# One decoder layer on one core: bias rows copied to the output early, the last token tile stored plainly, two chunks split ahead in the value product

## The chip, the cores and the metric

One core of one Trainium2 chip runs the whole layer. TensorE (PE) multiplies, VectorE (DVE), ScalarE (ACT) and GpSimd (POOL) work on tiles, SyncE (SP) issues most of the transfers; POOL issues those that add to what is already at the destination. The metric is the time of one execution in microseconds (us), the median of several; less is better.

## The reference

One layer: a mixer (dilated attention and a spatial gating unit), cross-attention into 256 memory tokens, and a SwiGLU block, each added to alpha times the stream and normalised. Width 2048, 512 tokens, hidden width 5632, all in float32. The change touches the end of the second part and the third:

```python
def _memory_cross_attention(h, mem, w_q, w_k, w_v, w_o):
    q = (h @ w_q).reshape(B, S, XATTN_HEADS, XATTN_HEAD_DIM)
    k = (mem @ w_k).reshape(B, M, XATTN_HEADS, XATTN_HEAD_DIM)
    v = (mem @ w_v).reshape(B, M, XATTN_HEADS, XATTN_HEAD_DIM)
    s = jnp.einsum('bshe,bmhe->bhsm', q, k).astype(jnp.float32) * (XATTN_HEAD_DIM ** -0.5)
    p = jax.nn.softmax(s, axis=-1)
    o = jnp.einsum('bhsm,bmhe->bshe', p.astype(v.dtype), v).reshape(B, S, D)
    return o @ w_o
...
    h = _layer_norm(DEEPNORM_ALPHA * h + xa, ln2_g[l], ln2_b[l])
    ff = (jax.nn.silu(h @ w_ffn_gate[l]) * (h @ w_ffn_up[l])) @ w_ffn_down[l]
    h = _layer_norm(DEEPNORM_ALPHA * h + ff, ln3_g[l], ln3_b[l])
```

## The kernel before

Every float32 product is made of three matmuls: each operand is split into a high part (a cast on ACT) and a low part (a subtraction on DVE), and high x high, high x low and low x high are added in PSUM. Weights come in chunks of 1 MB. All code is in one function; the order of the instructions on every engine is the order in which the program writes them, with small generators (a `Sched` that resumes them at every `tick()`) to interleave side work. Each engine runs its own instructions strictly in that order.

**The value product** (lines 1278 to 1315). The products of the memory's values with the output weights were made earlier and lie in DRAM (`vo_d`). So what is left of the cross-attention is a product of the attention weights `xpt` with 16 chunks, numbered 0 to 15 here: two halves of the tokens (`hf`), four column blocks (`cb`), two chunks each (`kb`). For a chunk c, `w_load` brings 1 MB into one of two raw buffers (`wraw`), and `w_split` makes two casts (line 199, into `whi`) and two subtractions (line 200, into `wlo`); `whi` and `wlo` have two buffers each. `next_w(c)` calls `w_ahead(c)`, which splits chunk c + 1 and loads c + 2 and c + 3, and only then come the 24 matmuls of chunk c (lines 235 to 237). Behind every second chunk two results are added to the residual on DVE (line 1307, the residual comes from DRAM into the single tile `Xa`) and their statistics taken (line 1308). After chunk 7 the first token half is normalised by `ln2(0)`: a chain of small DVE instructions (lines 382 to 385), then activations on ACT (line 1016) and POOL. `first_half` then transposes and splits that half (lines 1028 to 1049).

**SwiGLU.** Eleven blocks (j = 0 to 10) of 28 items each make the gate and up products by a seven-product (Strassen) scheme, P1 to P7, then six blocks make the down product. `Feed` keeps the weights coming: `pump` loads half-megabyte tiles `T` and `rt` on SP's queue up to 10 items ahead, `a` casts, `b` subtracts (lines 1198 and 1205) into one of four `ws` tiles; where a sum of two weight blocks is wanted, `b` lets POOL load the second block with an addition (line 1212). `prime` makes the first three of these splits, at the start of chunk 14 (line 1299).

**The end.** `gbs` (line 1546) loads the gain and bias rows of the last norm, repeated over 128 partitions, as soon as the tile of P2's operand is free, and then writes the bias rows four times into the output (line 1553), 1 MB each. The last results of P6 are added on DVE (line 1367) in the queue behind the last four splits, and PE's last two products (P7, P4) use P6's banks, so they wait for that. `final_ln` normalises a token tile on ACT (line 1541), multiplies by the gain on DVE (line 1542), and POOL adds the result onto the bias rows in DRAM (line 1543).

Of the kernel before, what the change touches and what calls it, by code (L numbers as in the profile page):

```python
# [17 lines left out]
P = 128  # L18
D = 2048
# [20 lines left out]
def layer_kernel(tc, x, mem, positions, ln_in_g, ln_in_b, w_in, sgu_norm_g, sgu_norm_b,  # L40
# [14 lines left out]
    def pool(name, stack=ctx, bufs=1, **kw):  # L55
        kw.setdefault("reuse_waits", "tile")
        if kw.get("space") == DRAM:
            kw.pop("reuse_waits")
        return stack.enter_context(tc.tile_pool(name=name, bufs=bufs, **kw))
# [9 lines left out]
    psa = pool("psa", space=PSUM)  # L69
    pst = ExitStack()  # L70
    psx = pool("psx", pst, space=PSUM)

    def acc():
        return psa.tile([P, 512], F32, name="acc", bufs=4)
# [108 lines left out]
    def w_tiles(c):  # L183
        if c < 21 and c % 3 == 2:
            q = [actp.tile([P, 2, 512], F32R, name=f"act{12 + j}").rearrange("p a b -> p (a b)") for j in range(4)]
            return q[:2], q[2:]
        hi = wp.tile([P, 2048], F32R, name="whi", bufs=2)
        lo = wp.tile([P, 2048], F32R, name="wlo", bufs=2)
        return ([hi[:, 0:1024], hi[:, 1024:2048]], [lo[:, 0:1024], lo[:, 1024:2048]])
# [21 lines left out]
    def w_ahead(c):  # L211
        w_load(c + 1)
        w_split(c + 1)
        if c < 19:
            w_load(c + 2)
            w_split(c + 2)
        w_load(c + 2)
        w_load(c + 3)
# [154 lines left out]
    def bcast(ap, n):  # L373
        return bass.AP(tensor=ap.tensor, offset=ap.offset, ap=[[0, P], [1, n]])
# [582 lines left out]


    phe = ExitStack()
    pf = [None, None]  # L960

    def open_e():
        ph.close()
# [45 lines left out]
    def ln2(hf):  # L1009
        ts = (2 * hf, 2 * hf + 1)  # L1010
        ln_chain(ts, stat2, mv2)
        for c in (0, 2, 1, 3):
            for t in ts:
                o = y2[t, c]
                if c < 2:
                    A.activation(o, o, AF.Identity, bias=mv2[:, t, 3:4], scale=mv2[:, t, 2:3])
                else:
                    G.tensor_scalar(o, o, mv2[:, t, 2:3], mv2[:, t, 3:4], op0=OP.mult, op1=OP.add)
        for c in range(4):
            for t in ts:  # L1020
                G.dma_start(y2n_d[t][c], y2[t, c])
# [219 lines left out]
                self.b()  # L1241
            self.pump()

    NR, NW = 4, 4
    feed = Feed()

    def half_rows(w, r, c0):
# [30 lines left out]
    for hf in range(2):  # L1278
        for cb in range(4):
            ps, rs = None, None  # L1280
            for kb in range(2):
                if kb == 0 and hf + cb == 0:
                    sched.need(lambda: 0 in xpt and 1 in xpt)
                if kb == 1 and hf + cb == 0:
                    sched.need(lambda: 2 in xpt and 3 in xpt)
                wh, wl = next_w(f"xo{hf}_{cb}", kb)
                if kb == 0:
                    ps = [acc() for _ in range(2)]
                if kb == (1 if hf + cb == 0 else 0):
                    if not y2:  # L1290
                        new_y2()
                    rs = zt("Xa")
                    for u in range(2):
                        nc.sync.dma_start(rs[:, u], res_d[1][2 * hf + u][:, cb * 512:cb * 512 + 512])
                    if hf == 1 and cb == 1:
                        feed.pump(4)
                    if hf == 1 and cb == 3:
                        feed.pump()
                        feed.prime()
                for i in range(2):  # L1300
                    t = 2 * hf + i
                    ts = slice(t * 128, t * 128 + 128)
                    for k in range(4):
                        x_ = xpt[(kb * 4 + k) // 2][:, k % 2]
                        mm3(ps[i], x_[:, 0, ts], x_[:, 1, ts], wh[:, k], wl[:, k], kb + k == 0, kb == 1 and k == 3)
                    if kb == 1:
                        V.tensor_tensor(y2[t, cb], ps[i], rs[:, i], OP.add)
                        V.bn_stats(stat2[:, t, cb], y2[t, cb])
                        if cb == 3 and i == 1:
                            ln2(hf)  # L1310
                            if hf == 0:
                                new_comb(A11)
                                new_comb(A12)
                                sched.spawn(first_half(), 4)
                    tick()
# [133 lines left out]
    for j in range(FB):  # L1449
        x = {}  # L1450

        def on(name, bk, j=j, x=x):
            def c11(bank_a, bank_d):
                for i in range(2):
                    V_ADD(x[1][:, i], bank_d[i], x[1][:, i])
                A.activation(x[1], x[1], AF.Silu)

            def x1(bank_a):
                x[1] = zt("Xa")
                for i in range(2):  # L1460
                    A.copy(x[1][:, i], bank_a[i])

            if name == "P1":
                x["A"] = bk
                if j:
                    x1(bk)
            elif name == "P2":
                if j == 0:
                    x1(x["A"])
                c11(x["A"], bk)  # L1470
                if 1 <= j <= 8:
                    sched.spawn(residual_task(j - 1), 1)
            elif name == "P5":
                x["H"] = zt("XH")
                x[5], x[12] = x["H"][:, 0:2], x["H"][:, 2:4]
                for i in range(2):
                    A.copy(x[5][:, i], bk[i])
            elif name == "P3":
                x["B"] = bk
            elif name == "P6":  # L1480
                x[2] = zt("Xb")
                for i in range(2):
                    A.copy(x[2][:, i], bk[i])

                def c12():
                    yield 1
                    for i in range(2):
                        V_ADD(x[12][:, i], x["B"][i], x[2][:, i])
                    V.tensor_tensor(x[12], x[12], x[1], OP.mult)
                    yield 2  # L1490
                    if j == FB - 1:
                        load_y("Xa", [(0, 0), (1, 0)])
                    x["fc"] = zt("FC")
                    yield from ff_first(j, x["fc"], x[12])
                sched.spawn(c12(), 0)
            elif name == "P7":
                for i in range(2):
                    V_ADD(x[2][:, i], bk[i], x[2][:, i])
                V_ADD(x[5], x[5], x[2])
            elif name == "P4":  # L1500
                for i in range(2):
                    V_ADD(x[2][:, i], bk[i], x[2][:, i])
                A.activation(x[2], x[2], AF.Silu)

                def rest():
                    V.tensor_tensor(x[5], x[5], x[2], OP.mult)
                    yield 2
                    yield from ff_second(j, x["fc"], x[5])
                sched.spawn(rest(), 1)
            if j == FB - 1:  # L1510
                next_group(0, name)

        def gate(name, c, j=j):
            if j == 0 and name not in ("P1", "P2"):
                sched.need(lambda: built[0] > c)
        product_block(*plan[j], on, gate if j == 0 else None)
# [18 lines left out]
    def final_ln(*ts):  # L1535
        ln_chain(ts, stat3, mv3)
        for c in (2, 3, 1, 0):
# [5 lines left out]
                G.dma_start(out[t * 128:(t + 1) * 128, z], o, accum_op=OP.add)  # L1543
            yield 1

    def gbs():
        yield 1
        for i, s_ in enumerate((ln3_g[0], ln3_b[0])):
            gb3.append(pf[0].tile([P, D], F32, name=f"c{A12}_{i}"))
            nc.sync.dma_start(gb3[i], bcast(s_, D))  # L1550
        yield 3
        for t in range(NT):
            nc.sync.dma_start(out[t * 128:(t + 1) * 128, :], gb3[1])

    for g in range(3):
        for nb in range(2):
# [48 lines left out]
            if last and nb:  # L1605
                cut = [o for o in order if o[0] in ("P7", "P4")]
                bank = product_block(n, order[:-len(cut)], on)
                assert feed.nb == len(feed.items)
                for name in ("P7", "P4"):
                    ws = [feed.next((name, c)) for c in range(n)]  # L1610
                    for i in range(2):
                        for c in range(n):
                            mm_item(bank["P6"], COMB[name], c, ws[c], False, c == n - 1, (i,))
                            if c < n - 1:
                                tick()
                        acc_y(2 + i, n1 if name == "P7" else n0, bank["P6"][i], True)
                        if name == "P4":
                            sched.spawn(final_ln(2 + i), 1)
                        tick()
            else:  # L1620
                product_block(n, order, on)
# [45 lines left out]
```

## Time and profile before

| | |
|---|---|
| Time, median of 3 runs | 2631.56 us (2630.79 to 2632.6) |
| The profiled execution: its own time | 2631.51 us |
| its span, first to last instruction | 2629.5 us |
| PE busy | 2550.6 us, 97% |
| DVE, ACT, POOL busy | 1726.2, 1104.4, 235.7 us |
| Mean granted TensorE clock | 0.989 of 2.4 GHz |

PE is the engine that sets the time: in the long middle of the kernel it has no gap at all. Its busy time is a sum of records that overlap (a matmul of 512 columns has a record of 0.39 us and a start every 0.227 us), so what is lost is better read from the starts than from the share.

### The profile page before, as it was taken

The numbers are of one execution on the slowest core, as the hardware profiler recorded it, in microseconds if no ns is written. First come the engines' busy times: TensorE is split into PE (matmuls) and PEld (weight loads), VectorE is DVE, ScalarE is ACT, GpSimd is POOL, SyncE is SP. The second block draws the span as 40 slices with busy tenths as digits, with TensorE's granted clock in tenths as the row PEclk, the third lists the DMA queues.
The fourth block names the chain that finished last, engine by engine and source line by source line (L and its number), as shares of the span: only waits on it lengthen the run. The fifth ranks groups of instructions, "written<-read, shape, count | busy, mean of one in ns | idle before, by whom it ended". The sixth has DMA issues, their size and how long they took to land.

```text
span 2629.5 us, 31646 instructions
## 1 busy us (share of the span) xinstructions
PE 2550.6 (97%) x12421; PEld 2146.8 (82%) x12421; DVE 1726.2 (66%) x2216; ACT 1104.4 (42%) x1370; POOL 235.7 (9%) x256
## 2 busy tenths in 40 slices
PE   8999999999999999998989999999999999999994
PEld 8999888888888888886778888888888877888883
DVE  4766556474535456435787777778777768787785
ACT  4464433233332134223655554545555544333432
POOL 1311000000000010001211111111110100000022
PEclk9999999999999999999999999999999999999997
DMA  8769722323334233425848888878888799887977
GB/s 295 235 202 306 220 80 81 96 66 108 87 105 181 96 112 113 150 91 180 260 118 230 236 242 245 202 224 225 234 239 240 202 348 304 286 273 224 287 195 168
DMA packets 271252, 511.80 MB, mean 195 GB/s; under 512 B 14464, under 2 KB 68992, under 8 KB 263680
## 3 DMA queue, kind: packets, MB, share of 16 engines
q1 hardware_dynamic: 223120, 411.15, 46.2%
q0 software_dynamic: 44336, 91.83, 17.6%
q10 hardware_dynamic: 3648, 6.82, 0.7%
q8 instruction: 97, 1.59, 0.2%
q14 instruction: 51, 0.42, 0.1%
HBM read 431.62 MB, written 78.12 MB: 194 GB/s over the span
## 4 chain that ended last, share of the span: by engine, by line
PE 43%; DMA 4%; DVE 4%; issue 2%; ACT 1%; POOL 1%; SPq 0%; POOLq 0%; DVEq 0%; ACTq 0%
PE acc L1342 10%; PE acc L1343 10%; PE acc L1341 10%; PE D L1342 4%; PE D L1343 4%; PE D L1341 4%; DMA Xa<-res_d 2%; DVE ws L1205 1%; PE aux L1396 1%; DMA T<-in_w_ffn_down_dram 1%; DVE wlo L200 1%; POOL out_dram L1543 1%; DMA rt<-in_w_ffn_gate_dram 0%; DVE T L1184 0%; DMA rt<-in_w_ffn_down_dram 0%
## 5 line engine op out<-in xcount | busy, mean ns | idle before, releaser
L200 DVE TENSOR_TENSOR wlo<-wraw,whi 128x1024 fp32r<-128x1024 f32 x258 | 305.1, 1225 | 264.1 <-ACT whi L199 263.8
L1198 ACT CAST ws<-T 128x1024 fp32r<-128x1024 f32 x263 | 275.7, 1054 | 395.4 <-PE acc L1343 110.8
L199 ACT CAST whi<-wraw 128x1024 fp32r<-128x1024 f32 x258 | 258.2, 1050 | 326.3 <-PE acc L237 195.5
L1205 DVE TENSOR_TENSOR ws<-T,ws 128x1024 fp32r<-128x1024 f32 x263 | 317.3, 1222 | 92.0 <-ACT ws L1198 91.6
L1205 DVE TENSOR_TENSOR ws<-rt,ws 128x1024 fp32r<-128x1024 f32 x195 | 237.9, 1222 | 80.9 <-ACT ws L1198 80.5
L1198 ACT CAST ws<-rt 128x1024 fp32r<-128x1024 f32 x195 | 205.0, 1054 | 187.8 <-PE acc L1343 145.6
L1343 PE MATMUL acc<-ws,big 128*128 128x512 f32 x528 | 207.1, 392 | 3.8 <-DVE big L1061 3.8
L1341 PE MATMUL acc<-ws,big 128*128 128x512 f32 x528 | 206.9, 392 | 2.1 <-ACT big L1058 2.1
L1342 PE MATMUL acc<-ws,big 128*128 128x512 f32 x528 | 206.8, 392 | 1.6 <-DVE ws L1205 1.5
L235 PE MATMUL acc<-whi,act 128*128 128x512 f32 x512 | 201.3, 393 | 0.0
L237 PE MATMUL acc<-whi,act 128*128 128x512 f32 x512 | 199.4, 390 | 0.0
L236 PE MATMUL acc<-wlo,act 128*128 128x512 f32 x512 | 199.2, 389 | 0.0
L235 PE MATMUL acc<-act,whi 128*128 128x512 f32 x384 | 152.0, 396 | 0.0
L237 PE MATMUL acc<-act,wlo 128*128 128x512 f32 x384 | 149.8, 390 | 0.0
L236 PE MATMUL acc<-act,whi 128*128 128x512 f32 x384 | 149.5, 389 | 0.0
L235 PE MATMUL acc<-memT,whi 128*128 128x256 f32 x432 | 122.4, 283 | 4.5 <-ACT whi L199 3.2
L237 PE MATMUL acc<-memT,wlo 128*128 128x256 f32 x432 | 122.0, 282 | 1.7 <-DVE wlo L200 1.6
L236 PE MATMUL acc<-memT,whi 128*128 128x256 f32 x432 | 121.1, 280 | 0.0
L1343 PEld LDWEIGHTS acc<-ws,big 128*128 128x128 f32 x528 | 99.9, 189 | 25.7 <-DVE big L1061 5.1
L1341 PEld LDWEIGHTS acc<-ws,big 128*128 128x128 f32 x528 | 99.8, 189 | 23.5 <-ACT big L1058 2.8
L1342 PEld LDWEIGHTS acc<-ws,big 128*128 128x128 f32 x528 | 99.8, 189 | 23.4 <-DVE ws L1205 2.7
L237 PEld LDWEIGHTS acc<-whi,act 128*128 128x128 f32 x512 | 96.1, 188 | 20.2
(396 smaller groups left out, 5952.9 us busy)
## 6 DMA issues: line engine op xcount, KB each, us to landing
rt<-in_w_ffn_gate_dram SPq DMA_DIRECT2D x88, 512.0 KB, 6.0
rt<-in_w_ffn_down_dram SPq DMA_DIRECT2D x82, 512.0 KB, 7.3
wraw<-in_w_in_dram SPq DMA_DIRECT2D x40, 1024.0 KB, 5.8
T<-in_w_ffn_gate_dram SPq DMA_DIRECT2D x44, 512.0 KB, 3.9
T<-in_w_ffn_up_dram POOLq DMA_DIRECT2D x44, 512.0 KB, 11.0
rt<-in_w_ffn_up_dram SPq DMA_DIRECT2D x44, 512.0 KB, 8.4
rt<-in_w_ffn_up_dram POOLq DMA_DIRECT2D x44, 512.0 KB, 6.2
wraw<-in_w_xv_dram SPq DMA_DIRECT2D x16, 1024.0 KB, 6.8
```

The source lines that it names most:

```text
L199: A.copy(hi[s], r[:, z])
L200: V.tensor_tensor(lo[s], r[:, z], hi[s].bitcast(F32), OP.subtract)
L235: T.matmul(o, lh, rh, start=start, stop=False)
L236: T.matmul(o, lh, rl, start=False, stop=False)
L237: T.matmul(o, ll, rh, start=False, stop=stop)
L1198: A.copy(e["ws"][:, 0], self.tiles[e["src"]])
L1205: V.tensor_tensor(e["ws"][:, 1], self.tiles[e["src"]], e["ws"][:, 0].bitcast(F32), OP.subtract)
L1341: T.matmul(bank[i], lh, rh, start=start and kk == 0, stop=False, skip_group_check=True)
L1342: T.matmul(bank[i], lh, rl, start=False, stop=False, skip_group_check=True)
L1343: T.matmul(bank[i], ll, rh, start=False, stop=stop and kk == 1, skip_group_check=True)
L1396: T.transpose(p[:, kk * 256 + i * 128:kk * 256 + i * 128 + 128], x[:, i, f * 128:f * 128 + 128], ident)
L1543: G.dma_start(out[t * 128:(t + 1) * 128, z], o, accum_op=OP.add)
```

## The change

Three things are altered. (1) The four writes of the bias rows at the end go away; instead SP copies the bias vector from DRAM, repeated 128 times, straight to three of the four row blocks of the output, one 1 MB transfer in each of the first three SwiGLU blocks, behind P2. (2) The fourth token tile gets its own closing function, `final_last`: gain and bias are both applied on chip (for two of the four column blocks DVE does it all in two instructions, for the other two ACT normalises first), and SP stores the result plainly. (3) In the value product, from chunk 1 on, `w_ahead` splits two chunks ahead, every third chunk into two of the `ws` tiles in place of `whi` and `wlo`; one more `w_ahead` stands in front of `ln2(0)`; and `prime` comes one chunk later.

```diff
@@ w_tiles
+        if c >= NCH - 14 and (c - NCH + 16) % 3 == 2:
+            t = [pf[0].tile([P, 2, 1024], F32R, name="ws", bufs=NW) for _ in range(2)]
+            return tuple([q[:, 0], q[:, 1]] for q in t)
@@ w_ahead
-        if c < 19:
+        if c < 19 or c >= NCH - 15:
             w_load(c + 2)
             w_split(c + 2)
@@ the value product
-                    if hf == 1 and cb == 3:
-                        feed.pump()
-                        feed.prime()
+                if hf == 1 and cb == 3 and kb == 1:
+                    feed.pump()
+                    feed.prime()
...
                         if cb == 3 and i == 1:
+                            if hf == 0:
+                                w_ahead(pos[0])
                             ln2(hf)
@@ SwiGLU blocks, behind P2
+                if j < 3:
+                    nc.sync.dma_start(out[j * 128:(j + 1) * 128, :], bcast(ln3_b[0], D))
@@ the end
+    def final_last(t):
+        ln_chain((t,), stat3, mv3)
+        rows = slice(t * 128, t * 128 + 128)
+        for c in (0, 1):
+            o = y[t, c]
+            A.activation(o, o, AF.Identity, bias=mv3[:, t, 3:4], scale=mv3[:, t, 2:3])
+        for c in (2, 0, 3, 1):
+            z = slice(c * 512, (c + 1) * 512)
+            o = y[t, c]
+            if c > 1:
+                V.scalar_tensor_tensor(o, o, mv3[:, t, 0:1], gb3[0][:, z], op0=OP.subtract, op1=OP.mult)
+                V.scalar_tensor_tensor(o, o, mv3[:, t, 2:3], gb3[1][:, z], op0=OP.mult, op1=OP.add)
+            else:
+                V.tensor_tensor(o, o, gb3[0][:, z], OP.mult)
+                V.tensor_tensor(o, o, gb3[1][:, z], OP.add)
+            nc.sync.dma_start(out[rows, z], o)
+        yield 1
...
-        yield 3
-        for t in range(NT):
-            nc.sync.dma_start(out[t * 128:(t + 1) * 128, :], gb3[1])
...
-                            sched.spawn(final_ln(2 + i), 1)
+                            sched.spawn(final_ln(2) if i == 0 else final_last(3), 1)
```

DVE at the start of the value product, before; `wlo<-wraw,whi` are splits (x2 is one chunk: first chunk 2, then 3 and 4), `Xb` and `XH` take the first and the second column block's results:

```order
L200 TENSOR_TENSOR wlo<-wraw,whi 128x1024 x2
L1307 TENSOR_TENSOR Xb<-acc,Xa 128x512
L1308 BN_STATS stat<-Xb 128x6
L1307 TENSOR_TENSOR XH<-acc,Xa 128x512
L1308 BN_STATS stat<-XH 128x6
L200 TENSOR_TENSOR wlo<-wraw,whi 128x1024 x4
L1307 TENSOR_TENSOR Xb<-acc,Xa 128x512
```

The same place now:

```order
L206 TENSOR_TENSOR ws<-wraw,ws 128x1024 x2
L206 TENSOR_TENSOR wlo<-wraw,whi 128x1024 x2
L1311 TENSOR_TENSOR Xb<-acc,Xa 128x512
L1312 BN_STATS stat<-Xb 128x6
L1311 TENSOR_TENSOR XH<-acc,Xa 128x512
L1312 BN_STATS stat<-XH 128x6
L206 TENSOR_TENSOR wlo<-wraw,whi 128x1024 x2
L206 TENSOR_TENSOR ws<-wraw,ws 128x1024 x2
L1311 TENSOR_TENSOR Xb<-acc,Xa 128x512
```

Chunk 3's split now stands in front of the first column block's additions instead of behind them, and so on for every second chunk. ACT around the first token half's norm, before (14 casts are chunks 2 to 8, the four behind the norm chunks 9 and 10):

```order
L199 CAST whi<-wraw 128x1024 x14
L1016 ACTIVATE Xb<-Xb,mv 128x512
L1016 ACTIVATE XH<-XH,mv 128x512
L1016 ACTIVATE Xb<-Xb,mv 128x512
L1016 ACTIVATE XH<-XH,mv 128x512
L199 CAST whi<-wraw 128x1024 x4
```

And now, from chunk 8 on:

```order
L205 CAST ws<-wraw 128x1024 x2
L205 CAST whi<-wraw 128x1024 x4
L1021 ACTIVATE Xb<-Xb,mv 128x512
L1021 ACTIVATE XH<-XH,mv 128x512
L1021 ACTIVATE Xb<-Xb,mv 128x512
L1021 ACTIVATE XH<-XH,mv 128x512
L205 CAST ws<-wraw 128x1024 x2
```

The casts of chunks 9 and 10 moved in front of the norm's activations; chunk 11 is the first behind them. The end of SP's queue, before (`c_0` and `c_1` are the gain and bias rows):

```order
L1550 DMA c_0_18904<-in_ln_g_dram 128x2048
L1550 DMA c_1_18906<-in_ln_b_dram 128x2048
L1553 DMA out_dram<-c_1_18906 128x2048 x4
```

And now:

```order
L1576 DMA c_0_18907<-in_ln_g_dram 128x2048
L1576 DMA c_1_18909<-in_ln_b_dram 128x2048
L1569 DMA out_dram<-FC 128x512
L1569 DMA out_dram<-XH 128x512
L1569 DMA out_dram<-FH 128x512
L1569 DMA out_dram<-Xb 128x512
```

The four 1 MB writes are gone; the four stores of 256 KB are the last token tile's.

## Rows read from the trace of the kernel before

**Rows 1.** PE's waits over the span: us in total, times, longest.

```profile
PE acc L1341 <- DVE FC L1367: 18.8, 1, 18.8
PE acc L235 <- ACT whi L199: 8.7, 2, 5.5
PE acc L236 <- DVE wlo L200: 6.3, 6, 2.9
```

**Rows 2.** Three stretches: length, busy per engine, granted clock, DMA share, GB/s.

```profile
1186.30:1289.20 102.90, 91.03 (x397) 72.62 (x395) 62.76 (x91) 46.97 (x61) 9.82 (x14) 0.95 0.63 219
...
1370.00:1448.00 78.00, 78.00 (x355) 64.75 (x354) 59.87 (x58) 39.73 (x43) 9.60 (x8) 1.00 0.83 229
...
2572.40:2591.30 18.90, 0.08 (x1) 0.00 (x0) 5.49 (x6) 4.09 (x4) 0.00 (x0) 0.59 0.81 235
```

**Rows 3.** PE in the value product: start, length, instruction, [idle before <- releaser].

```profile
1172.52 0.39 PE L235 MATMUL acc<-whi,big 128*128 128x512 f32 x1
...
1177.74 0.39 PE L237 MATMUL acc<-whi,big 128*128 128x512 f32 x1
...
1200.52 0.79 PE L236 MATMUL acc<-wlo,big 128*128 128x512 f32 x1 [2.86 <-DVE wlo L200]
...
1240.80 0.79 PE L235 MATMUL acc<-whi,big 128*128 128x512 f32 x1 [5.46 <-ACT whi L199]
...
1245.81 0.27 PE L1034 MATMUL aux<-ident,Xb 128*128 128x128 f32 x1
1245.92 0.27 PE L1034 MATMUL aux<-ident,XH 128*128 128x128 f32 x1
```

**Rows 4.** DVE in the same stretch.

```profile
1188.23 2.36 DVE L200 TENSOR_TENSOR wlo<-wraw,whi 128x1024 fp32r<-128x1024 f32 x2
1196.60 0.69 DVE L1307 TENSOR_TENSOR Xb<-acc,Xa 128x512 f32<-128x512 f32 x1 [6.01 <-DMA Xa<-res_d]
...
1199.26 4.62 DVE L200 TENSOR_TENSOR wlo<-wraw,whi 128x1024 fp32r<-128x1024 f32 x4
```

**Rows 5.** ACT around the first norm.

```profile
1236.88 0.81 ACT L1016 ACTIVATE Xb<-Xb,mv 128x512 f32<-128x512 f32 x1 [11.09 <-DVE mv L385]
...
1239.71 3.88 ACT L199 CAST whi<-wraw 128x1024 fp32r<-128x1024 f32 x4
```

**Rows 6.** The raw buffers in the value product, twelve loads of 1 MB.

```profile
DMA to landing us min/median/max: 4.8/6.8/12.6
```

**Rows 7.** PE at the end.

```profile
2572.10 0.39 PE L1343 MATMUL acc<-ws,big 128*128 128x512 f32 x1
2591.33 0.77 PE L1341 MATMUL acc<-big,wraw 128*128 128x512 f32 x1 [18.85 <-DVE FC L1367]
```

**Rows 8.** Transfers, 2564.5 to 2588: queue, packets, MB, share; issue, KB, us to landing.

```profile
q0 software_dynamic: 1293, 2.48, 57.5%
q1 hardware_dynamic: 576, 4.19, 44.4%
...
T<-in_w_ffn_down_dram POOLq DMA_DIRECT2D x1, 512.0 KB, 23.9
```

**Rows 9.** The same view, 2584 to 2586.

```profile
q0 software_dynamic: 212, 0.41, 112.6%
```

**Rows 10.** DVE at the end.

```profile
2590.50 0.68 DVE L1367 TENSOR_TENSOR FC<-acc,FC 128x512 f32<-128x512 f32 x1
...
2616.61 0.16 DVE L385 SCALAR_TENSOR_TENSOR mv<-mv 128x1 f32<-128x1 f32 x1
...
2619.77 0.69 DVE L1542 TENSOR_TENSOR XH<-XH,c 128x512 f32<-128x512 f32 x1
```

**Rows 11.** DVE's two-operation form, line 1381: ns min/median/max.

```profile
L1381 DVE SCALAR_TENSOR_TENSOR FH<-FH x16: 683/686/690, 1426.1 to 1976.8; 128x512 f32<-128x512 f32 x16
```

**Rows 12.** Issues of 256 KB: the last addition to the output, a plain store alone.

```profile
out_dram<-XH POOLq DMA_DIRECT2D x1, 256.0 KB, 6.9
...
y2n_d<-Xb POOLq DMA_DIRECT2D x1, 256.0 KB, 2.3
```

More of the change, by code (lines that the diff above doesn't have):

```diff
@@ L71, in layer_kernel @@
     psx = pool("psx", pst, space=PSUM)
+    NR, NW = 4, 4
+    pf = [None, None]
     def acc():
@@ L959, in layer_kernel @@
     phe = ExitStack()
-    pf = [None, None]
     def open_e():
@@ L1242, in after @@
             self.pump()
-    NR, NW = 4, 4
     feed = Feed()
```

## The prediction

> **What bounds the kernel now.** PE does. I read its waits first, sorted by length [rows 1]: one of 18.8 us, where PE waits for DVE's last addition of P6, and several in the value product, for a cast (`whi`) or a subtraction (`wlo`). Then the stretches [rows 2]: in a SwiGLU block (1370 to 1448) PE has no gap in 78 us while the transfer engines are 0.83 busy, so there only something that makes PE wait can cost; in the value product (1186.3 to 1289.2) the granted clock is 0.95; in the gap at the end PE is still and the transfers are busy. So three places can move: the value product, the gap at the end, and what follows PE's last matmul. The profiled execution took 2631.51 us, 2.0 more than its span, and stands 0.05 us from the median of 2631.56, so sums against it are sums against the median. About 0.2%, 5 us, is what a measurement of this kernel can tell from no change.
>
> **Value product: what is lost.** Chunk 0 starts its matmuls at 1172.52, and the last of its 24 starts at 1177.74 [rows 3]: 23 steps of 0.227 us, so a chunk is 5.45 us. From 1186.3 the 15 others need 81.7 us, and the 32 transposes of `first_half`, 0.11 us apart [rows 3], 3.5 us: 85.2 of 102.9 us [rows 2]. Lost: 17.7 us. The two long waits [rows 3] carry most. At 1200.52 chunk 3 waits for its low part; DVE had to do the first column block's additions before it, and these waited 6.01 us for the residual [rows 4]. Chunk 3 could have started its second matmul at 1186.3 + 2 x 5.45 + 0.2 = 1197.4, so 3.1 us, and the matmuls behind it run at the lower clock level (0.63 us records in place of 0.39), some 1.5 more: 4.6. At 1240.80 chunk 9 waits for its cast, which stands on ACT behind the norm's activations, which wait for DVE's chain [rows 5]: 5.46 us of idle, which with the overlapping record is 5.6, about 1 more for the low part, and again slow matmuls, 1.4: 8.0. The rest, 5.1 us, is in six short waits for a low part.
>
> **What the change gives there.** Chunk 3's subtraction now follows chunk 2's directly: chunk 2's end at 1188.23 + 2.36 = 1190.6 [rows 4], chunk 3's at 1193.0, and PE wants it at 1197.4; that wait goes. Chunk 4's subtraction now stands behind the first additions, which end near 1196.6 + 2.7 = 1199.3 as before; it is done by 1201.7, its first half by 1200.5, and PE wants chunk 4 at 1202.6: 2 us to spare. Chunks 9 and 10 are cast before the norm's activations. DVE makes chunk 10's low part (2.36 us) before the norm's chain, so the chain ends that much later, but PE then has chunks 8, 9 and 10, 16.3 us of work, and chunk 11 needs only what lies in between: 2.4 for that low part, 2.2 of chain, 3.2 of activations [rows 5], 2.3 of cast and subtraction, together 10. That wait goes too. The short waits should go where raw data is there in time; the last chunks' loads run beside 2 MB of first SwiGLU weights and one took 12.6 us [rows 6], so I leave half of the 5.1 in place. Gain: 4.6 + 8.0 + 2.5 = 15 us, between 8 (the first rival) and 17.7. `prime` at chunk 15 costs nothing that I can find: its third cast waits for chunk 14's matmuls, with chunk 15's 5.45 us of PE work as cover; without that cover it would cost a cast and a subtraction, 2.3 us. The new tiles add no instruction, only other addresses. The matmuls after the product start earlier by the same shift, with the same lead of DVE and ACT, so the waits near 1314 to 1330 stay.
>
> **The gap at the end.** PE stops after the matmul at 2572.10 and starts at 2591.33 [rows 7]. It waits for the addition at 2590.50 [rows 10], which stands behind the last split, and that one waits for the last weight tile, added by POOL's queue: issued at 2564.3, landed 23.9 us later [rows 8], at 2588.2. From 2564.5 to 2588 that queue (q0) moved 2.48 MB while SP's queue (q1) moved 4.19 MB, the four writes of bias rows, at 44% of the engines [rows 8]. Near the end q0 is alone and moves 0.41 MB in 2 us [rows 9], 0.205 MB/us, with the engines full. Without the four writes its 2.48 MB takes 12.1 us; it ends at 2576.6 where it ended near 2586.8 (the landing comes about 1.5 later in both). Fully: 10.2 us earlier. I take 9.6, since the load of the bias rows itself stays and the first tiles were already under way; the bounds are 3 (the second rival) and 11. Everything behind, up to the last norm, moves with it. The gap that stays, over 9 us, is still long enough for the clock: it fell to 0.59 in the gap [rows 2] and PE's restart is at the lower level [rows 7]; I count that loss as unchanged.
>
> **After the last matmul.** The last norm's chain ends at 2616.77 [rows 10]. Before, four multiplications follow (the last at 2619.77, 0.69 us), then POOL's additions, the last one issued at 2620.9 and landed 6.9 later [rows 12], and 1.7 us to the end of the span. Now DVE does eight instructions in place of four, the two-operation form at 0.686 [rows 11], the other at 0.69: first of a pair to second 0.72, pair to pair 1.33, so 5.4 us, to 2622.2 (no wait for ACT at the start, where 0.9 us lay: 2619.77 less three of 0.69 is 2617.7). Then one plain store: alone, such a transfer landed in 2.3 [rows 12]; I take 3.0 for it behind three others, and 1.7 to the end: 2626.9 against 2629.5. Gain 2.5 us; bounds +3.5 (2.3 and a shorter last store) and -1.3 (a landing of 6.9 as now).
>
> The Trainium skill speaks against this part: "DMA: Bandwidth & Descriptors", section "Issuing engines are not separate DMA queues", says that transfers run on the same 16 engines whoever issues them, so that moving them from POOL to SP saves only issue time. By that rule alone the stores would keep their 6.9 us, the four extra DVE instructions would cost, and the sum below would come out 3.8 us higher. The trace differs in kind, not in issuer: 2.3 us for the plain store above was issued by POOL too.
>
> **The three copies in the SwiGLU blocks.** SP issues each 1 MB copy without waiting for anything; behind it on its queue stand the residual's loads (j = 1, 2) or the next weights (j = 0). No transfer from DRAM to DRAM is in the trace. The nearest rows are loads of 1 MB, 4.8 to 12.6 us to landing [rows 6], and a block leaves 17% of 78 us, 13 us, of the transfer engines free [rows 2]. So I price them at nothing; the cover is that free share. If it were gone, each copy would cost its transfer time less 13 us.
>
> **The sum.** 2631.5 - 15 - 9.6 - 2.5 = 2604.4.
>
> **The rivals.** *Two raw buffers become the bound (2612).* A buffer is loaded, cast (0.97 until its first half is there [rows 5]), subtracted (2.36) and freed: landing + 3.5 us with the steps between, and it must come round every two chunks, 10.9 us. That holds up to a landing of 7.4; the median is 6.8, the longest 12.6 [rows 6], and the same bytes now have to move in 87 in place of 103 us. At 9 us each pair loses 1.6, six pairs 9.6, and the gain shrinks to 7 or 8. *The added loads are slow by themselves (2611).* If q0 gained only 3 us at the end from the writes' absence, the sum is 6.6 higher. For it: the share of q0 is 57.5% beside them, more than half. Against it: the rate when alone [rows 9]. *The norm keeps its wait (2613):* chunk 10's cast waits for chunk 7's matmuls and its low part for that cast, the norm's chain for both; if chunk 11's raw data is late too, most of the 8 us moves from chunk 9 to chunk 11. For it: 10 of 16.3 us are spoken for. This is also the case that the change doesn't do what it says there. *Slower than before (2656):* the copies from DRAM to DRAM are slow and hold SP's queue. The kernel breaks even when a copy takes 13 + 27/3 = 22 us; at 30 us, three copies would cost 51 and the sum be 2656. For it: nothing like it is in the trace. Against it: 22 us is far above every landing of 1 MB here.
>
> **How the numbers follow.** Forecast 0.66, rivals 0.14, 0.10, 0.06 and 0.04. The likeliest time is 2604.4. From below, all of 17.7, 11 and 3.5 gives 2599; two us are for the waits behind the product, which I took as unchanged: 2597. Above, the three milder rivals end at 2611 to 2613, so 2614 leaves out the slow copies and mixtures. Faster by over 0.2%: 0.95, all cases but the last; within: 0.01; slower: 0.04.
>
> **What would show it.** In the changed kernel PE should have no wait above 1 us in the value product and the granted clock there 1.00; the 18.8 us wait should be 9 to 10; the last weight tile should land some 14 us after its issue; from the last norm's chain to the end of the span should be about 10 us (12.7 now); blocks 0 to 2 should show no new wait of PE. If casts in the value product wait for the raw loads and PE for them, the first rival holds; if the tile still lands after 20 us, the second; if PE waits at chunk 11 behind the norm, the third; if it waits in blocks 0 to 2, the last.

## The result

The changed kernel takes 2601.93 us (median of 4 runs, 2600.34 to 2605.89) against 2631.76 for the kernel before in the same runs: a ratio of 0.9889, 95% interval 0.9872 to 0.9906, so 1.1% or about 29 us less (the two medians lie 29.8 apart). Forecast were 2604.4 with a range of 2597 to 2614. The profiled execution took 2602.38 us with a span of 2600.4.

PE's waits in the changed kernel, sorted as in [rows 1] (us in total, times, longest):

```profile
PE acc L1347 <- DVE FC L1373: 9.0, 1, 9.0
PE aux L457 <- DMA act<-in_mem_dram: 6.3, 1, 6.3
PE acc L1348 <- DVE ws L1210: 3.8, 4, 1.3
PE acc L1349 <- DVE big L1066: 3.4, 3, 2.3
PE acc L241 <- ACT whi L205: 3.0, 1, 3.0
PE aux L1402 <- DVE XH L1497: 2.1, 1, 2.1
PE aux L1402 <- DVE XH L1514: 1.7, 1, 1.7
```

The wait of 18.8 us is 9.0, and no wait of the value product is among the long ones any more; it had 5.5 us for `whi` and 2.9 for `wlo`. (The 3.0 us for `whi` that is left lies at the kernel's start, before 11.21 us.) The stretches that answer to [rows 2], with the same columns: the value product, a SwiGLU block (the second, with its copy), and the gap at the end:

```profile
1185.40:1270.80 85.40, 85.39 (x394) 70.76 (x393) 61.59 (x88) 46.75 (x61) 8.45 (x13) 1.00 0.70 246
1353.30:1431.30 78.00, 78.00 (x354) 64.75 (x353) 59.86 (x59) 39.64 (x42) 9.60 (x8) 1.00 0.86 243
2557.70:2566.60 8.90, 0.00 (x0) 0.00 (x0) 5.48 (x6) 4.08 (x4) 0.00 (x0) 0.67 0.52 96
```

In the value product PE has no gap and the clock is at its upper level (1.00); nor has it one in the block, whose transfer share rose from 0.83 to 0.86. PE's last matmul of that product, its restart at the end, and DVE's last steps (beside [rows 3], [rows 7] and [rows 10]):

```profile
1270.74 0.39 PE L243 MATMUL acc<-whi,big 128*128 128x512 f32 x1
2566.64 0.77 PE L1347 MATMUL acc<-big,wraw 128*128 128x512 f32 x1 [8.96 <-DVE FC L1373]
2565.81 0.68 DVE L1373 TENSOR_TENSOR FC<-acc,FC 128x512 f32<-128x512 f32 x1
2591.70 0.16 DVE L391 SCALAR_TENSOR_TENSOR mv<-mv 128x1 f32<-128x1 f32 x1
2596.72 0.69 DVE L1568 TENSOR_TENSOR Xb<-Xb,c 128x512 f32<-128x512 f32 x1
```

And the transfers that the sum spoke of: the last weight tile (here [rows 8] had 23.9), the last plain store ([rows 12] had 6.9 for the adding one), and a copy from DRAM to DRAM in the second SwiGLU block (KB, us to landing):

```profile
T<-in_w_ffn_down_dram POOLq DMA_DIRECT2D x1, 512.0 KB, 14.0
out_dram<-Xb SPq DMA_DIRECT2D x1, 256.0 KB, 2.0
out_dram<-in_ln_b_dram SPq DMA_DIRECT2D x1, 1024.0 KB, 7.2
```

**Where the 29.1 us of the two profiled executions lie.** The same instructions are taken in both traces and their distance followed along the kernel. PE's last transposes in front of the value product start 0.9 us earlier, before anything that the change touches. The product itself, from there to its last matmul, takes 85.9 us (1184.85 to 1270.74) in place of 102.9: 17.0 gained. By DVE's sum behind P6 in the first SwiGLU block (`XH<-acc,Xb`, 1362.25 before, 1346.28 after) 2.0 are given back; by the same sum of the last block (2147.82, 2132.92) another 1.1. The wait at the end gives 9.9 (18.85 to 8.96), the stretch from PE's restart to the last norm's chain 0.2, and what follows the chain 4.2 (2616.77 to 2629.5 was 12.7; 2591.86 to 2600.4 is 8.5). 0.9 + 17.0 - 2.0 - 1.1 + 9.9 + 0.2 + 4.2 = 29.1.

### The profile page after: what moved, and what is told of

It is laid out like the page before. It is cut to its first block, busy times and chain, and to the rows that moved or that the text cites. A ratio compares the mean times of both kernels' runs of the same rounds, so it can differ in the third digit from the quotient of the medians.

```text
span 2600.4 us, 31653 instructions
## 1 busy us (share of the span) xinstructions
PE 2546.7 (98%) x12421; PEld 2145.9 (83%) x12421; DVE 1728.3 (66%) x2220; ACT 1101.3 (42%) x1368; POOL 231.8 (9%) x252
## 4 chain that ended last, share of the span: by engine, by line
PE 48%; DVE 3%; DMA 2%; ACT 1%; issue 1%; SPq 0%; ACTq 0%; DVEq 0%
PE acc L1349 11%; PE acc L1348 11%; PE acc L1347 11%; PE D L1347 4%; PE D L1349 4%; PE D L1348 4%; DMA T<-in_w_ffn_down_dram 1%; PE acc L243 1%; PE acc L242 1%; PE acc L241 1%; DVE ws L1210 1%; PE aux L1402 1%; DMA rt<-in_w_ffn_gate_dram 0%; DVE T L1189 0%; ACT ws L1203 0%
## 5 line engine op out<-in xcount | busy, mean ns | idle before, releaser
L206 DVE TENSOR_TENSOR wlo<-wraw,whi 128x1024 fp32r<-128x1024 f32 x248 | 293.5, 1225 | 261.9 <-ACT whi L205 261.9
L205 ACT CAST whi<-wraw 128x1024 fp32r<-128x1024 f32 x248 | 248.0, 1049 | 308.9 <-PE acc L243 183.4
```

The lines of the kernel that those rows point to most:

```text
L205: A.copy(hi[s], r[:, z])
L206: V.tensor_tensor(lo[s], r[:, z], hi[s].bitcast(F32), OP.subtract)
```

## The parts one by one

All times are medians; the kernel before ran beside each group (2633.27, 2632.98 and 2631.97 us).

| run | time, us | ratio to before | 95% interval |
|---|---|---|---|
| e1, only the value product | 2616.95 | 0.9944 | 0.9932 to 0.9956 |
| e2, three writes at the end | 2610.36 | 0.9916 | 0.9902 to 0.9930 |
| e3, last tile added | 2605.70 | 0.9899 | 0.9886 to 0.9913 |
| e4, last stores by POOL | 2602.70 | 0.9894 | 0.9879 to 0.9909 |
| e5, no split before the norm | 2603.16 | 0.9887 | 0.9873 to 0.9900 |
| e6, one chunk ahead | 2609.81 | 0.9917 | 0.9903 to 0.9930 |
| e7, copies six times | 2649.88 | 1.0063 | 1.0051 to 1.0076 |
| e8, P6's sums first | 2601.70 | 0.9886 | 0.9872 to 0.9899 |
| e9, norm behind P7 too | 2597.30 | 0.9866 | 0.9852 to 0.9879 |
| e10, as e9, gain on POOL | 2599.15 | 0.9884 | 0.9868 to 0.9900 |
| e11, copies in block 0 | 2603.58 | 0.9889 | 0.9876 to 0.9903 |

**e1.** The value product alone; copies, `final_last` and the missing writes are undone:

```diff
-                if j < 3:
-                    nc.sync.dma_start(out[j * 128:(j + 1) * 128, :], bcast(ln3_b[0], D))
...
+        yield 3
+        for t in range(NT):
+            nc.sync.dma_start(out[t * 128:(t + 1) * 128, :], gb3[1])
...
-                            sched.spawn(final_ln(2) if i == 0 else final_last(3), 1)
+                            sched.spawn(final_ln(2 + i), 1)
```

> Only the value product is changed; the four writes of bias rows at the end, the additions for all four token tiles and no copies in the SwiGLU blocks are as before. Parts that add up: the value product takes 86 us in place of 103, some 1.2 are given back at once in the stage behind it and 1 more in the last SwiGLU block, so 15 us are left: 2616.5 (2615 to 2618), with PE's wait at the end still 18 to 20 us and 12.7 us from the last norm's chain to the end of the span. Rival, the parts depend on each other (reaching the end earlier changes what the adding loads meet there): the wait at the end differs from 18.8 by over 3 us and the time is near 2609 or 2622.

Measured 2616.95. The value product and the gap at the end (columns as above):

```profile
1187.70:1272.80 85.10, 85.10 (x394) 70.78 (x393) 61.72 (x88) 46.75 (x61) 8.59 (x13) 1.00 0.70 247
2559.60:2578.60 19.00, 0.04 (x1) 0.07 (x1) 5.56 (x6) 4.08 (x4) 0.00 (x0) 0.61 0.80 231
```

The gap stays 19.0 us with the transfers 0.80 busy, though the kernel reaches it some 13 us earlier. So the parts add up, and the gain in the value product is worth half of the whole: 0.56% of 2631.76 is 14.7 us. From the last norm's chain to the end of the span it is 13.6 us (2604.46 to 2618.0), 0.9 beyond the 12.7 expected: the last adding store took 7.5 us to land, before 6.9.

**e2.** The bias rows of three row blocks written at the end again, the last tile as in the changed kernel:

```diff
-                if j < 3:
-                    nc.sync.dma_start(out[j * 128:(j + 1) * 128, :], bcast(ln3_b[0], D))
...
+        yield 3
+        for t in range(3):
+            nc.sync.dma_start(out[t * 128:(t + 1) * 128, :], gb3[1])
```

> The changed kernel, with the bias rows of the first three row blocks written from the chip at the end as before and no copies in the SwiGLU blocks. Shared transfer engines (my reason): 3.15 of 4.19 MB are back, so three quarters of the 9.9 us: PE's wait at the end 9.0 + 7.4 = 16.4 us, the last weight tile lands some 21 us after its issue in place of 14, time 2609.3. Rival, the adding loads are slow by themselves and the wait was shortened by something else: wait 9 to 11 us, time 2602 to 2604.

Measured 2610.36; PE's wait, and the last weight tile (KB, us to landing):

```profile
PE acc L1347 <- DVE FC L1373: 15.8, 1, 15.8
```

```profile
T<-in_w_ffn_down_dram POOLq DMA_DIRECT2D x1, 512.0 KB, 20.8
```

3.15 MB of plain writes cost 6.8 us of wait (15.8 less 9.0), four of them 9.9: about 2.2 to 2.4 us for each MB. That is the loss that shared engines would give, in step with the bytes, and the rival (slow by themselves, a wait of 9 to 11 us) is out. Yet the rival is not wrong about the transfers: without the writes the adding loads have the engines to themselves and still move 0.205 MB/us. The view of the transfers of the changed kernel, from 2549.5 to 2560.5, with only that queue:

```profile
q0 software_dynamic: 1171, 2.27, 112.7%
```

**e3 and e4.** The last tile closed like the others, with a fourth copy to bring its bias rows; and the plain stores issued by POOL:

```diff
-                if j < 3:
+                if j < 4:
...
-                            sched.spawn(final_ln(2) if i == 0 else final_last(3), 1)
+                            sched.spawn(final_ln(2 + i), 1)
```

> The changed kernel, but the fourth token tile is closed as the others are (ACT, one multiplication on DVE, POOL adds to bias rows that a fourth copy brought). My reason, an adding store lands later than a plain one: landing 6 to 7 us in place of 2.0, less the four DVE instructions: time 2605 to 2606, and 12 to 12.7 us from the last norm's chain to the end of the span in place of 8.5. Rival, by the rule that transfers cost the same whoever issues them: the four extra DVE instructions (2.9 us) are saved and the store is no slower, time 2599 to 2601.

```diff
-            nc.sync.dma_start(out[rows, z], o)
+            G.dma_start(out[rows, z], o)
```

> The changed kernel, with the four plain stores of the last token tile issued by POOL in place of SP. If the kind of the transfer decides (plain or adding): landing 2.0 to 2.5 us, from the last norm's chain to the end 8.5 to 9.2 us, time within 1 us of the changed kernel's 2601.9. Rival, POOL's queue itself is slow: landing 5 to 7 us, time 2605 to 2607.

Measured 2605.70 and 2602.70. The last transfer of each, e3 first (KB, us to landing):

```profile
out_dram<-XH POOLq DMA_DIRECT2D x1, 256.0 KB, 7.4
```

```profile
out_dram<-Xb POOLq DMA_DIRECT2D x1, 256.0 KB, 2.4
```

From the last norm's chain to the end of the span e3 needs 13.2 us (2592.67 to 2605.9), e4 9.9 (2588.52 to 2598.4), the changed kernel 8.5. Adding costs the most: POOL issues both, and the plain one lands in 2.4 us. But the issuer is not free. e4's chain-to-end is 1.4 us longer than the changed kernel's and 0.7 beyond what was expected, though its time is within 1 us of the changed kernel's. From DVE's end it is 0.3 us more until the store is issued, 0.3 more until it lands, and 0.7 more from the landing to the end of the span: that last piece is 1.65 us, much as in e3 and in the kernel before (1.66), and 0.9 in the changed kernel, where SP issues the store. What fills that time was not tried.

The prediction weighed a sentence of the Trainium skill ("DMA: Bandwidth & Descriptors", "Issuing engines are not separate DMA queues"). It says that transfers run on the same 16 engines whoever issues them, and that issuing from several engines saves only the time of issuing. The trace of e4, where the issuer alone is changed, agrees as to the landing (2.4 us, 2.0 from SP), but the whole difference is 1.4 us, of which 0.3 lie before the issue. On e3, where the kind is changed, the sentence says nothing.

**e5 and e6.** The changed kernel without the split in front of the norm, and with one chunk ahead but with that split:

```diff
-                            if hf == 0:
-                                w_ahead(pos[0])
                             ln2(hf)
```

> The changed kernel without the one extra split (chunk 10) in front of the first token half's norm. By the prediction's count the stretch behind the norm needs about 10 us until the next chunk's low part is there (less 2.4, since chunk 10's own low part no longer stands in front of the chain, plus its cast and subtraction behind the norm), and two chunks, 10.9 us, are in hand: PE waits 0 to 1.5 us at chunk 10, time 2602 to 2604. Rival, this one call carries the 8.0 us of chunk 9: a wait of 4 to 6 us at chunk 10 and a time of 2607 to 2610.

```diff
-        if c >= NCH - 14 and (c - NCH + 16) % 3 == 2:
+        if False:
...
-        if c < 19 or c >= NCH - 15:
+        if c < 19:
```

> The changed kernel splitting one chunk ahead as before, without the two borrowed tiles, but with the extra split (now chunk 9) in front of the norm. By the prediction's count chunk 3's 4.6 us and the short waits' 5.1 come back and chunk 9's 8.0 do not: 2611 to 2612, with a wait of some 3 us at chunk 3. Rival 1, two ahead is needed behind the norm as well: all 15.8 us come back, 2617. Rival 2, the call in front of the norm carries nearly all of the gain: 2603 to 2606.

e5 took 2603.16, no different from the changed kernel, and its value product 85.6 us (1184.67 to 1270.30) has no wait of PE above 0.25 us. With two chunks in hand the extra call is worth nothing. e6 took 2609.81, 1.2 us under its range. PE's waits above 0.3 us in its value product (1184.69 to 1282.07, 97.4 us):

```profile
1199.32 0.50 PE L242 MATMUL acc<-wlo,big 128*128 128x512 f32 x1 [2.70 <-DVE wlo L206]
1223.98 0.50 PE L242 MATMUL acc<-wlo,big 128*128 128x512 f32 x1 [0.45 <-DVE wlo L206]
1235.61 0.50 PE L242 MATMUL acc<-wlo,big 128*128 128x512 f32 x1 [0.41 <-DVE wlo L206]
1239.70 0.33 PE L1039 MATMUL aux<-ident,Xb 128*128 128x128 f32 x1 [1.31 <-ACT Xb L1021]
1240.41 0.33 PE L1039 MATMUL aux<-ident,XH 128*128 128x128 f32 x1 [0.38 <-ACT XH L1021]
1276.95 0.50 PE L242 MATMUL acc<-wlo,big 128*128 128x512 f32 x1 [1.01 <-DVE wlo L206]
```

Chunk 3's wait and the short ones are back as counted, the 5.46 us for chunk 9's cast are not. One thing was not counted: PE now reaches the transposes of `first_half` before the norm's activations are done (1239.70), since the low part of chunk 9 stands on DVE in front of the norm's chain; these two waits are 1.7 us. With one chunk ahead the extra call gives 5.5 us (102.9 to 97.4); two ahead gives 11.5 more and makes it superfluous.

## The copies, and what is left of the wait at the end

**e7 and e11.** Each copy six times; and all three copies in the first block:

```diff
                 if j < 3:
-                    nc.sync.dma_start(out[j * 128:(j + 1) * 128, :], bcast(ln3_b[0], D))
+                    for _ in range(6):
+                        nc.sync.dma_start(out[j * 128:(j + 1) * 128, :], bcast(ln3_b[0], D))
```

> The changed kernel with each of the three copies of bias rows made six times in its block (18 MB in place of 3). The work hidden in free transfer time: one copy raised the share of its block from 0.83 to 0.86 or 0.87, about 2.6 us of all engines, so six need 16 of the 13 us that are free: share near 1.0 in blocks 0 to 2, and a loss of 0 to 5 us per block, time 2602 to 2617. Rival, the copies hold SP's queue one after the other, 7 us each as the landings are: 35 us more per block during which weights wait, time above 2640.

e7 took 2649.88, 48 us more than the changed kernel. Its SP queue in the second block, and PE's waits over the span:

```profile
1396.79 35.00 SPq L1481 DMA_DIRECT2D out_dram<-in_ln_b_dram  x6
1431.96 0.47 SPq L1380 DMA_DIRECT2D FH<-in_ln_g_dram  x1
```

```profile
PE D L1348 <- DVE ws L1210: 38.9, 3, 18.4
```

The rival held, with its 35 us; why the copies hold the queue it left open. The six copies of a block write the same rows, and each is issued only when the one before has landed (1396.79, landed 1405.81; the next at 1405.83). So SP's queue stands still for 35 us, the weights behind it come late, and PE waits three times: 2.2, 18.3 and 18.4 us. That prices a hold of SP's queue, not a copy: in the second and third block some 17 of 35 us are covered and 18 are waited for; the first block covers more. Hence e11:

```diff
-                if j < 3:
-                    nc.sync.dma_start(out[j * 128:(j + 1) * 128, :], bcast(ln3_b[0], D))
+                if j == 0:
+                    for t in range(3):
+                        nc.sync.dma_start(out[t * 128:(t + 1) * 128, :], bcast(ln3_b[0], D))
```

> The changed kernel with its three copies of bias rows all in the first SwiGLU block, to three different row blocks, one issued behind the other. In e7 each copy wrote the same rows as the one before, waited for its landing and so held SP's queue for 35 us. If that wait and not the transfers was the cost: the queue is held for about 1 us, the block's transfer share rises from 0.83 to 0.91 to 0.94, PE waits for nothing new there, time 2601 to 2603. Rival, copies are slow in themselves: PE waits 3 us or more in block 0, time 2605 to 2610.

Measured 2603.58, 0.6 us above its range, and on SP's queue, for three copies to different rows:

```profile
1311.02 2.04 SPq L1481 DMA_DIRECT2D out_dram<-in_ln_b_dram  x3
```

The hold is 2.0 us, about 1 was expected, and PE has no new wait there. The copies run from 1311 to 1325, where the transfer engines are little used (in the kernel before a share of 0.20 from 1312 to 1332 and 0.34 from 1332 to 1342), so the next block still has 0.83 and not 0.91 to 0.94. The copies are free as placed, one in each block, and three are free at that spot; three in a full block were not tried.

**e8.** The changed kernel still loses 9.0 us at the end, because P6's last sums stand on DVE behind the last four splits. They need only P6's matmuls:

```diff
-            feed.after()
+            hold = first and name == "P6" and c > 0
+            if not hold:
+                feed.after()
             if c == n - 1:
                 on(name, bank[name])
+            if hold and c == n - 1:
+                feed.after()
+                feed.after()
```

(`first` is set for the last block alone.)

> The changed kernel, with DVE's last additions of P6 written in front of the last four splits in place of behind them (same work, other order on DVE). If the rest of the wait at the end is only a place in DVE's queue: the additions run when P6's matmuls end, the wait of 9.0 us falls to about 1, the granted clock stays up and gives 1 to 2 us more: time 2592 to 2594. Rival, the wait moves to the splits that PE needs next (P7's third, then P4's, whose last tile lands 14 us after its issue): 3 us gained at most, 2599 to 2601.

Measured 2601.70: neither. PE goes on at once and runs all of P7, and then waits in front of P4:

```profile
2572.01 0.76 PE L1347 MATMUL acc<-c,wlo 128*128 128x512 f32 x1 [7.60 <-ACT Xa L1554]
...
2567.05 2.81 DVE L1555 TENSOR_TENSOR FC<-FC,c 128x512 f32<-128x512 f32 x4 [0.76 <-ACT FC L1554]
2569.87 1.40 DVE L1555 TENSOR_TENSOR XH<-XH,c 128x512 f32<-128x512 f32 x2
2571.18 0.68 DVE L1378 TENSOR_TENSOR FC<-acc,FC 128x512 f32<-128x512 f32 x1
```

The profile names ACT, which is among those that P4's start follows; what came last on PE's side is the last of these rows, P7's first sum, which frees the bank that P4 writes. It stands behind the norm of the first two token tiles and six multiplications by the gain. So the wait had a second one behind it, again a place in a queue.

**e9.** On top of e8, the norm's chain behind the first of the four splits, its multiplications behind P7's two sums:

```diff
                     if last and nb:
-                        sched.spawn(final_ln(0, 1), 1)
+                        feed.b()
+                        ln_chain((0, 1), stat3, mv3)
+                        sched.spawn(final_ln(0, 1, chain=False), 7)
                         return
```

> As e8, and the gain multiplications of the first two token tiles are written behind P7's two sums on DVE (their norm's chain behind the first of the last four splits). If all of the rest of the wait is place in DVE's queue: P7's first sum runs behind the last split and not behind six multiplications that wait for ACT, PE waits at most 1.5 us in front of P4 in place of 7.6, the clock stays up, PE ends near 2574, and DVE's own work (about 24 us from the last split on) sets the end: time 2592 to 2595. Rival, DVE's work or the adding stores of 3 MB that stand on POOL's queue set the end whatever PE does: 2598 to 2601.

Measured 2597.30, its profiled execution 2596.07. In the tail PE waits once, and DVE's work sets the end:

```profile
2567.45 0.47 PE L1347 MATMUL acc<-c,wlo 128*128 128x512 f32 x1 [0.83 <-DVE FC L1378]
...
2589.40 0.69 DVE L1574 TENSOR_TENSOR Xb<-Xb,c 128x512 f32<-128x512 f32 x1
```

The mechanism is the expected one and the time 2 us above its range, that of the profiled execution 1.1. Of that the trace shows 0.9: the last plain stores meet adding stores of the tiles before and land in 3.0 to 5.2 us in place of 2.0 to 2.4, so from DVE's end to the end of the span it is 3.9 us in place of 3.0. It is the lowest time measured, 4.6 us under the changed kernel and 6.3 under e11 in the same group; its interval (0.9852 to 0.9879) overlaps that of the changed kernel.

**e10.** On top of e9, half of those multiplications on POOL:

```diff
-                V.tensor_tensor(o, o, gb3[0][:, z], OP.mult)
+                (G if not chain and t == 1 else V).tensor_tensor(o, o, gb3[0][:, z], OP.mult)
```

> As e9, with four of the eight gain multiplications of the first two tiles on POOL in place of DVE (2.8 us less on DVE). If DVE's work sets the end by then: 2.5 us less than e9, 2589.5 to 2592.5. Rival, POOL is slow at it and its adding stores come so much later that they end last: no gain on e9, or a loss of up to 4 us, with the last landing of an adding store at the end of the span.

Measured 2599.15, no gain on e9. From P7's first sum to DVE's end it is 29.0 us (2563.62 to 2592.61) in place of 23.5. The rival named the wrong place, though: the adding stores do not end last, DVE does. DVE and POOL side by side:

```profile
2567.45 2.58 DVE L1556 TENSOR_TENSOR XH<-XH,c 128x512 f32<-128x512 f32 x1
2569.96 0.67 DVE L1593 TENSOR_TENSOR FC<-FC,acc 128x512 f32<-128x512 f32 x1
...
2574.07 2.47 DVE L273 SCALAR_TENSOR_TENSOR rs_c<-mv,rs_c 128x1 f32<-128x1 f32 x1
2576.57 0.16 DVE L275 SCALAR_TENSOR_TENSOR mv<-rs_c,mv 128x1 f32<-128x1 f32 x1
...
2567.85 1.63 POOL L1556 TENSOR_TENSOR FC<-FC,c 128x512 f32<-128x512 f32 x1
...
2574.62 1.89 POOL L1556 TENSOR_TENSOR XH<-XH,c 128x512 f32<-128x512 f32 x1
```

Four times a DVE instruction lasts until POOL's multiplication is over; one on a single column takes 2.47 us in place of 0.22. The four lose 7.9 us, the moved multiplications save 2.4, which is the 5.5 us.

## Why the prediction came out right, step by step

**Value product, -15 forecast: the sum right, by two misses that happen to cancel.** The stretch gave 17.0 of the 17.7 lost. The step that left half of the short waits in place was too careful: it took a late raw load for a wait of PE. The loads are late, and ACT waits for them seven times in the value product of the changed kernel (who sat idle for what, on tile `wraw`):

```profile
  DMA wraw<-vo_d: 25.5, 7
```

but PE has two chunks, 10.9 us, in hand and never waits. So the first rival saw a real bound and missed the cover. The other miss is "the waits near 1314 to 1330 stay", by which the stage behind the product was to keep the whole shift. 2.0 us go back in that stage, the first SwiGLU block, where a new wait of 0.51 us for the first split of the weights appears at 1277.31 and the clock after its waits is lower (us, PE busy, granted clock, transfer share, GB/s; before, then now):

```profile
1312.00:1332.00 20.00, 13.18 (x45) 0.86 0.20 49
1295.30:1315.30 20.00, 14.07 (x45) 0.73 0.32 100
```

How much goes back differs between executions. From the product's last matmul to the sum behind P6 it is 73.6 us in the one trace before (1288.70 to 1362.25) and 75.5 here (1270.74 to 1346.28); the nine other traces with two chunks ahead (e7 left out, for its copies hold up this stage) have 74.1 (e4) to 76.1 (e1). Why the clock is lower there was not tried. The 1.1 us of the last SwiGLU block are no loss that the change is shown to cause. From the sum behind P6 in the block before to that of the last it is 83.8 us before (2064.01 to 2147.82) and 84.9 here (2048.04 to 2132.92), but 83.8 again in e8 (2047.68 to 2131.49), which has the same instructions up to there; PE's wait of 2.1 us for `XH`, 1.1 before, is 1.1 in e8 too. The net gain of e1 is 14.7. The third part, `prime` one chunk later, was not run by itself; the 0.51 us is all that the trace shows of it.

**Chunks 9 and 10 before the norm: the mechanism half right.** The wait went, and none came up at chunk 11, so the third rival is out; but e5 shows that two chunks ahead does it alone.

**The gap, -9.6: right.** 9.9, with the tile landing 14.0 us after its issue as worked out. With four writes put back the wait is 19.0 (e1), with three 15.8 (e2). The clock after the restart costs what it did: 25.2 us from there to the norm's chain, 25.4 before.

**After the last matmul, -2.5: too small, past its bound of 3.5.** 4.2 us. DVE's eight instructions took 5.6 us, 5.4 were counted (2591.77 to 2597.41). The term that was off is the landing: 2.0 us for the last store where 3.0 was taken "behind three others", and 1.0 in place of 1.7 behind it. The prediction took both from stores that POOL issues and put nothing on the issuer. With POOL as the issuer (e4) the gain is 2.8 (9.9 in place of 12.7), nearly the forecast; the other 1.4 came with SP. e3 gives the other side: four adding stores, 1 MB on a queue that moves 0.205 MB/us, are 5.1 us of transfer alone.

**The copies, 0: right.** Landings of 6.0 to 7.2 us and no wait of PE in blocks 0 to 2 that it did not have before, but for the 0.51 us at 1277.31, which lies ahead of the first copy (1310.21). The price if the cover were gone was put somewhat too high: a block carries a hold of some 17 us of SP's queue (e7), not 13.

## What to carry to other kernels

A transfer that adds to its destination moved 0.205 MB/us here with all engines full, so near the end of a kernel take other traffic from beside it and let the last result leave by a plain store (from SP: with POOL as its issuer the end took 1.4 us longer). Where PE waits for an addition, read what stands before that addition on its engine: here neither the data nor the arithmetic was late, only its place, and behind the first such place stood a second. Splitting two chunks ahead turned late loads and a norm in the middle into nothing, and made a special call for the worst place unnecessary.

## What the runs showed of the hardware

While POOL multiplied two tiles in SBUF (1.89 us), a DVE instruction of 0.22 us took 2.47 and ended with POOL's (e10). The Trainium skill says so ("SBUF — State Buffer", "SBUF: two separate sides"): VectorE with two SBUF inputs and GpSimd take turns at one pair of ports, and the later one waits out the other's instruction. The trace agrees that they take turns. It doesn't show that the later one waits: in three of the four cases DVE's record starts 0.4 to 0.55 us before POOL's (2574.07 and 2574.62 above), and DVE is held all the same.

The store that ends the kernel was followed by 0.9 us to the end of the span when SP issued it, and by 1.65 when POOL issued the same store (e4).

A copy of 1 MB from a vector in DRAM, repeated 128 times, to DRAM landed in 6.0 to 7.2 us, and three issued together in 10.0 (median, e11); the loads of 1 MB in the value product took 4.8 to 12.6 ([rows 6]).
